# Two plain gate tiles, a delayed overwrite of an activation sum, and transposes inside the first branch, in a hybrid decoder layer

## The chip, the cores and the metric

The kernel runs on one NeuronCore of one Trainium2 chip. The metric is the device time of one execution in microseconds (us). The engines named below are PE (matrix multiplication, with PEld for its weight loads), DVE and ACT (elementwise work; both read PSUM), POOL (elementwise work on SBUF) and SP, which here only issues DMAs.

## What is computed

One inference step of one decoder layer for 1024 prompt tokens and 64 sample tokens, 1088 columns in all, with a model width of 1024. Cut to what matters here:

```
proj = rms_norm(x) @ w_in              # holds, among others, g_a and g_b (1024 columns each)
h_m  = mLSTM branch (512 wide)         h_a = sliding-window attention branch (512 wide)
mix  = sigmoid(g_a) * (h_m @ w_branch_a) + sigmoid(g_b) * (h_a @ w_branch_b)
x    = x + mix @ w_out
x    = x + (silu(hf @ w_gate) * (hf @ w_up)) @ w_down      # hf = rms_norm(x)
```

The four stages the change touches are, in order of time: the gates g_a and g_b, the merge of the two branches, and the projection by `w_out` with the preparation of the feed-forward part.

## The kernel before

Every fp32 operand is held as a high and a low part (`XH`, `XL` for the activations, `wh`, `wl` for weights), so one product is three matmuls (`product`, L158). Activations lie as [128, 8, 1088]: eight blocks of 128 features, 1088 tokens. The tokens are cut in two halves of 544 (`first`, `second`), and each half into pieces of 256 and 288 columns (`halves`).

**Gates (L1042 to L1107).** There are eight gate tiles of 128 columns, m = 0 to 7, each for both branches. Tile 0 is computed plainly: for each branch and half, two pieces of 24 matmuls, 192 in all. Tiles 1 to 7 use a seven-product scheme (Strassen's, in Winograd's form) in place of eight: `times` (L1000) issues 12 matmuls for each piece of each product, so 168 a tile. The scheme needs sums of activation blocks. With a11, a12 the two feature halves of the first token half and a21, a22 those of the second, they are S1 = a21 + a22, S2 = S1 - a11, S3 = a11 - a21 and S4 = a12 - S2. The loop at L1063 makes them in four quarters of 136 columns and splits each into high and low parts. S2 to S4 go to tiles of their own (`SH`, `SL`, shown as SHG, SLG); S1 overwrites a21 in `XH`, `XL` (L1068). That write must wait for the plain tile's reads of the same columns, and it is the first split of its quarter. `right_sides` (L978) makes seven weight sums a tile from two raw loads, and `right` (L971) splits each into a slot of the tags `wh` and `wl`, which have four slots each. A gate result goes through tanh on ACT and is stored to DRAM (`TG`).

**Merge (L1109 to L1172).** `merge_all(1)` multiplies the attention output (features 0 to 3 of `XH`) with `w_branch_b`, 8 tiles of three chunks (384, 352, 352 columns) of 12 matmuls, and DVE multiplies with the gate. Then nine tiles of the mLSTM output are loaded from DRAM (`VED`) into `ve` (three buffers), transposed on PE (four transposes each, into one of two `tp` buffers of PSUM), copied by ACT to the high part and subtracted by DVE to the low part (L1159 to L1169). `merge_all(0)` then does for the mLSTM branch what `merge_all(1)` did for the other; POOL adds the two.

**Projection and preparation (L1208 to L1310).** Each token tile is multiplied with `w_out` in four column groups of 256. For groups 2 and 3, `project_rows` (L1231) uses one PSUM tile each, one DVE add (L1209) and one ACT square with its sum (L1210). `norm_rows` (L1235), `turn` (L1264) and `combine` (L1249) follow: they normalise, transpose and make the sums of the feed-forward part's own seven-product scheme.

The order on each engine outside the two hand-ordered early parts (L561, L563) is not the order of the text. A planner sets it when the program is built: it simulates the engines in time, and takes among the instructions that it believes ready, by and large, the one earliest in the text. On the chip each engine then runs its list strictly in that order, and SP issues all DMAs from one list.

Of the kernel before, what the change touches and what calls it, by code (L numbers as in the profile page):

```python
# [9 lines left out]
F32 = mybir.dt.float32  # L10
F32R = mybir.dt.float32r
I32 = mybir.dt.int32
AF = mybir.ActivationFunctionType
ALU = mybir.AluOpType
AX = mybir.AxisListType
PSUM = bass.MemoryType.PSUM

P = 128
D = 1024
KD = D // P  # L20
# [4 lines left out]
TILES = [(t, t * P, min(P, T - t * P)) for t in range((T + P - 1) // P)]  # L25
# [49 lines left out]
def hybrid_kernel(ctx: ExitStack, tc: tile.TileContext, i, o):  # L75
# [15 lines left out]
    def f32(ap):  # L91
        return ap.bitcast(F32)
# [25 lines left out]
    def split(hi, lo, raw, pin=False):  # L118
        ins = S.copy(hi, raw)  # L119
        if pin:  # L120
            tc.keep_in_program_order(ins)
        V.tensor_tensor(lo, raw, f32(hi), op=ALU.subtract)  # L122
# [31 lines left out]
    def load_tile(w, c0, kt=8, n=P, **kw):  # L154
        hi, lo = load_w([(w_rows(w, 0, kt, c0, n), 0, n)], kt, n, **kw)
        return [(hi[:, k], lo[:, k]) for k in range(kt)]
# [36 lines left out]
    def by_feature(out, c0, cn, ws, xh, xl):  # L193
        product(out, [(ws[k], (xh[:, k, c0:c0 + cn], xl[:, k, c0:c0 + cn])) for k in range(len(ws))])
# [829 lines left out]
    def f544(a):  # L1024
        return a[:, 256:800]
# [10 lines left out]
    def gate_tiles(m):  # L1036
        return [MIX[:, x, HALF * (m % 2):HALF * (m % 2) + HALF] for x in range(4)]

    def store_gate(branch, m, h, w):
        nc.sync.dma_start(TG[branch, m, :, HALF * h:HALF * h + HALF], w)  # L1040

    ws = [load_tile(i["w_in"], c0) for c0 in (GA, GB)]  # L1042
    w4 = gate_tiles(0)
    for branch in range(2):
        for h in range(2):
            a = ag.tile([P, 1024], F32, tag="ag", name="pg")
            for cs in halves:
                by_feature(a[:, 256 + cs.start:256 + cs.stop], HALF * h + cs.start, cs.stop - cs.start, ws[branch], XH, XL)
            w = w4[2 * branch + h]
            S.activation(w, f544(a), AF.Tanh, scale=0.5)  # L1050
            store_gate(branch, 0, h, w)

    CQ = HALF // 4
    quarters = [slice(CQ * n, CQ * n + CQ) for n in range(4)]
# [1 line left out]
    def whole(q, half, cs, out=None):  # L1056
        c = slice(HALF * half + cs.start, HALF * half + cs.stop)
        if out is None:
            out = cg.tile([P, 4, CQ], F32, tag="cg", name="cg")
        V.tensor_tensor(out, f32(XH[:, q, c]), f32(XL[:, q, c]), op=ALU.add)  # L1060
        return out

    for cs in quarters:  # L1063
        c = slice(HALF + cs.start, HALF + cs.stop)
        s3 = whole(q0, 1, cs, MIX[:, 0:4, c])
        s2 = whole(q1, 1, cs)
        V.tensor_tensor(s2, s3, s2, op=ALU.add)
        split(XH[:, q0, c], XL[:, q0, c], s2)  # L1068
        a11 = whole(q0, 0, cs)
        V.tensor_tensor(s2, s2, a11, op=ALU.subtract)  # L1070
        split(SH[:, 0, :, cs], SL[:, 0, :, cs], s2)
        V.tensor_tensor(s3, a11, s3, op=ALU.subtract)
        split(SH[:, 1, :, cs], SL[:, 1, :, cs], s3)
        s4 = whole(q1, 0, cs)
        V.tensor_tensor(s4, s4, s2, op=ALU.subtract)
        split(SH[:, 2, :, cs], SL[:, 2, :, cs], s4)

    def gate_sides():
        for m in range(1, 8):
            yield from right_sides(*load_gates(m))  # L1080

    HH, HL = XH[:, q0], XL[:, q0]
    left, sides, ready = left_sides(), gate_sides(), []
    for m in range(1, 8):
        outs, (w1, w2, w3, sg) = {}, gate_tiles(m)
        for n in range(7):
            w = take_side(sides, ready)
            if BANKS[n] not in outs:
                outs[BANKS[n]] = ag.tile([P, 1024], F32, tag="ag", name="pg")
            a = outs[BANKS[n]]  # L1090
            for cs in halves:
                times(a[:, 256 + cs.start:256 + cs.stop], left[n], w, FRESH[n], cs)
            sums(n, {b: f544(x) for b, x in outs.items()}, w1, w2, w3)
            if n == 2:
                S.activation(sg, f544(a), AF.Tanh, scale=0.5)
                store_gate(0, m, 0, sg)
            elif n >= 4:
                x = (w3, w2, w1)[n - 4]
                S.activation(x, x, AF.Tanh, scale=0.5)
                store_gate(int(n < 6), m, int(n != 5), x)  # L1100
            if m == 7 and n < 2:
                for cs in quarters:
                    c = slice(HALF * n + cs.start, HALF * n + cs.stop)
                    split(HH[:, :, c], HL[:, :, c], HA[:, :, c])
# [19 lines left out]
    def merge_all(branch, xh, xl):  # L1124
        for m in range(8):
            th = gp.tile([P, T], F32, tag="gth", name="gth", bufs=4)
            nc.sync.dma_start(th[:], TG[branch, m])
            if m % 2 == 0:
                if branch:
                    raw = load_b(m * P)  # L1130
                    hi = wp.tile([P, WT], F32R, tag="wh", name="wh")
                    lo = wp.tile([P, WT], F32R, tag="wl", name="wl")
                    split(hi[:, :1024], lo[:, :1024], raw[:, :1024])
                    h3 = hi[:, :1024].rearrange("p (k n) -> p k n", k=4)
                    l3 = lo[:, :1024].rearrange("p (k n) -> p k n", k=4)
                else:
                    h3, l3 = load_w([(w_rows(i["w_branch_a"], 0, 4, m * P, 256), 0, 256)], 4, 256)
            ms = slice((m % 2) * P, (m % 2) * P + P)
            wm = [(h3[:, k, ms], l3[:, k, ms]) for k in range(4)]
            for c0, cn in CHUNKS:  # L1140
                pb = acc.tile([P, 512], F32, tag="acc", name="pb")
                by_feature(pb[:, :cn], c0, cn, wm, xh, xl)
                mx, tc_ = MIX[:, m, c0:c0 + cn], th[:, c0:c0 + cn]
                if branch:
                    V.scalar_tensor_tensor(mx, tc_, 1.0, pb[:, :cn], op0=ALU.add, op1=ALU.mult)
                else:
                    V.scalar_tensor_tensor(tc_, tc_, 1.0, pb[:, :cn], op0=ALU.add, op1=ALU.mult)
                    G.tensor_tensor(mx, mx, tc_, op=ALU.add)

    ves = []  # L1150
    for t, r0, nt in TILES:
        ve = gp.tile([P, 4, P], F32, tag="ve", name="ve", bufs=3)
        nc.sync.dma_start(ve[:nt], VED[t, 0:nt])
        ves.append(ve)
        if t == 2:
            break
    merge_all(1, HH, HL)
    HH, HL = XH[:, q1], XL[:, q1]
    for t, r0, nt in TILES:  # L1159
        if t < len(ves):  # L1160
            ve = ves[t]
        else:
            ve = gp.tile([P, 4, P], F32, tag="ve", name="ve", bufs=3)
            nc.sync.dma_start(ve[:nt], VED[t, 0:nt])
        tp = ptp.tile([P, 4, P], F32, tag="tp", name="tp")
        for h in range(4):
            PE.transpose(tp[:, h, :nt], ve[:nt, h], ident[:nt, :nt])
        S.copy(HH[:, :, r0:r0 + nt], tp[:, :, :nt])
        V.tensor_tensor(HL[:, :, r0:r0 + nt], tp[:, :, :nt], f32(HH[:, :, r0:r0 + nt]), op=ALU.subtract)  # L1169
    merge_all(0, HH, HL)  # L1170
    for c in (close_ptp, close_acc, close_gp):
        c()  # L1172

# [1 line left out]
    def col(t):  # L1175
        return t * P + (HALF - 4 * P if t >= 4 else 0)
# [54 lines left out]
    def project_rows(t, u):  # L1231
        nt = TILES[t][2]
        add_rows(t, u, wu[u - 2], x2s[t][:nt, 256 * u:256 * u + 256], nt)

    def norm_rows(t):  # L1235
        _, r0, nt = TILES[t]
        x2 = x2s.pop(t)
        ss, y, a = (np_.tile([P, 1], F32, tag=n, name=n, bufs=2)[:nt] for n in ("ns", "ny", "na"))
        V.tensor_reduce(ss, ss4[:nt, t], axis=AX.X, op=ALU.add)
        S.activation(y, ss, AF.Ln, scale=1.0 / D, bias=eps[:nt])  # L1240
        S.activation(y, y, AF.Exp, scale=-0.5)
        V.tensor_scalar(ss, ss, -0.5 / D, -0.5 * EPS, op0=ALU.mult, op1=ALU.add)
        V.tensor_scalar(a, y, y, ss, op0=ALU.mult, op1=ALU.mult)
        V.tensor_scalar(y, a, 1.5, y, op0=ALU.add, op1=ALU.mult)
        xns[t] = nq.tile([P, D], F32, tag="xn", name="xn", bufs=2)
        norm_apply(x2, xns[t], nfw, nt, y)
        nc.sync.dma_start(X2D[r0:r0 + nt, 512:D], x2[:nt, 512:D])
# [47 lines left out]
    for n, t in enumerate(rows[:7]):  # L1295
        if n + 3 < len(rows):
            load_rows(rows[n + 3])
        for u in (2, 3):
            project_rows(t, u)
        norm_rows(t)  # L1300
        if n >= 2:
            turn(rows[n - 2])
# [225 lines left out]
```

## Time and profile before

| what | value |
|---|---|
| median of 3 runs | 1528.57 us (1527.46 to 1529.47) |
| profiled execution, its own time | 1530.48 us |
| span of the profile (first to last instruction) | 1528.5 us |
| PE busy | 1470.6 us, 96% of the span, 10430 matmuls |
| DVE busy | 801.6 us, 52% |
| ACT busy | 511.6 us, 33% |
| POOL busy | 249.0 us, 16% |
| mean granted TensorE clock | 0.991 |

PE's busy share is made of modelled matmul ends and hides how densely the matmuls follow one another, so stretches are better judged by how many matmuls they hold. The profile's 40 slices are 38.2 us each. The gates run from 386.7 to 576.0 us, the merge from 576.0 to 683.1 us, the projection and the preparation from there to about 816 us.

### The profile page before, as it was taken

What the parts mean: (1) busy time and instruction counts of PE and PEld (TensorE: products, weight loads), DVE (VectorE), ACT (ScalarE), POOL (GpSimd) and SP (SyncE); (2) the same over time, 40 slices, a digit from 0 to 9 for tenths busy, and PEclk for the clock granted to TensorE, in tenths of its full rate; (3) what the DMA queues carried; (4) which work ended last, traced back from release to release, by engine and by line L of the source; (5) the groups of instructions that cost most, each with busy time, mean ns of one, the idle gap of its engine ahead of it and who ended that gap; (6) DMA issues with size and microseconds to landing.
All of it is one profiled execution on the core that took longest, in us unless ns stands there. A gap on an engine that the chain in (4) does not pass through costs nothing.

```text
span 1528.5 us, 25750 instructions
## 1 busy us (share of the span) xinstructions
PE 1470.6 (96%) x10430; PEld 1382.0 (90%) x10430; DVE 801.6 (52%) x1515; ACT 511.6 (33%) x1059; POOL 249.0 (16%) x359
## 2 busy tenths in 40 slices
PE   6999999999979999899999999999999999999998
PEld 5887799888879999899999999999999998888887
DVE  6877525477764453444596555555555563325221
ACT  5666433321333341223463222223222242224110
POOL 1211100235101100140143222112221110000000
PEclk9999999999979999999999999999999999999999
DMA  8100113112313336334422233223232246536440
GB/s 259 37 15 11 49 55 84 55 44 56 99 57 114 90 122 224 124 103 144 157 87 83 73 85 86 84 66 109 80 85 85 72 153 195 176 131 217 139 127 18
DMA packets 171372, 154.91 MB, mean 101 GB/s; under 512 B 21746, under 2 KB 145074, under 8 KB 171254
## 3 DMA queue, kind: packets, MB, share of 16 engines
q1 hardware_dynamic: 171254, 153.27, 32.6%
q8 instruction: 82, 1.34, 0.4%
q14 instruction: 36, 0.29, 0.1%
HBM read 118.55 MB, written 34.70 MB: 100 GB/s over the span
## 4 chain that ended last, share of the span: by engine, by line
PE 83%; DVE 7%; ACT 3%; DMA 3%; issue 1%; POOL 1%; SPq 0%; DVEq 0%; ACTq 0%; POOLq 0%
PE pf L1005 27%; PE pg L1005 9%; PE ad L1481 6%; PE ad L1480 6%; PE acc L161 5%; PE ad L1483 5%; PE acc L163 5%; PE acc L162 5%; PE pb L161 2%; PE pb L162 2%; PE pb L163 2%; PE po L460 1%; PE sc L408 1%; DVE wl L122 1%; ACT pp L428 1%
## 5 line engine op out<-in xcount | busy, mean ns | idle before, releaser
L161 PE MATMUL acc<-wh,XH 128*128 128x256 f32 (+1 forms) x640 | 185.6, 290 | 1.7 <-ACT va L333 1.1
L163 PE MATMUL acc<-wh,XL 128*128 128x256 f32 (+1 forms) x640 | 182.5, 285 | 0.6 <-DVE XL L1193 0.6
L162 PE MATMUL acc<-wl,XH 128*128 128x256 f32 (+1 forms) x640 | 182.4, 285 | 0.0
L119 ACT CAST wh<-raw 128x512 fp32r<-128x512 f32 (+2 forms) x108 | 81.7, 762 | 211.2 <-PE pf L1005 88.5
L1005 PE MATMUL pf<-XH,wh 128*128 128x288 f32 (+1 forms) x688 | 138.5, 289 | 1.0 <-DVE w L1018 0.9
L1005 PE MATMUL pf<-XH,wl 128*128 128x256 f32 (+1 forms) x656 | 131.9, 288 | 0.0
L161 PEld LDWEIGHTS acc<-wh,XH 128*128 128x128 f32 x640 | 123.5, 193 | 6.7 <-issue 3.9
L163 PEld LDWEIGHTS acc<-wh,XL 128*128 128x128 f32 x640 | 123.4, 193 | 0.8 <-DVE XL L1193 0.8
L162 PEld LDWEIGHTS acc<-wl,XH 128*128 128x128 f32 x640 | 123.4, 193 | 0.0
L1005 PEld LDWEIGHTS pf<-XH,wh 128*128 128x128 f32 x688 | 111.2, 189 | 1.5 <-DVE w L1018 1.5
L1005 PEld LDWEIGHTS pf<-XH,wl 128*128 128x128 f32 x656 | 106.1, 188 | 0.0
L1005 PE MATMUL pf<-SH,wl 128*128 128x288 f32 (+1 forms) x512 | 102.3, 288 | 0.0
L1005 PE MATMUL pf<-XL,wh 128*128 128x256 f32 (+1 forms) x344 | 99.3, 289 | 0.0
L1005 PE MATMUL pf<-SH,wh 128*128 128x256 f32 (+1 forms) x496 | 99.0, 288 | 0.0
L1005 PE MATMUL pf<-XL,wl 128*128 128x288 f32 (+1 forms) x328 | 94.6, 289 | 0.0
L1337 POOL TENSOR_TENSOR w<-w,w 128x544 f32<-128x544 f32 x21 | 37.4, 1781 | 299.2 <-ACT w L1336 284.7
L122 DVE TENSOR_TENSOR SL<-kraw,SH 128x1536 fp32r<-128x1536 f32 (+1 forms) x24 | 39.8, 1658 | 83.2 <-ACT SH L119 83.2
L1481 PE MATMUL ad<-XL,SH 128*128 128x512 f32 x214 | 83.3, 389 | 0.0
L1480 PE MATMUL ad<-XH,SH 128*128 128x512 f32 x214 | 83.3, 389 | 0.0
L122 DVE TENSOR_TENSOR wl<-raw,wl 128x512 fp32r<-128x512 f32 x61 | 53.2, 874 | 57.3 <-ACT wl L119 57.3
L1005 PEld LDWEIGHTS pf<-SH,wl 128*128 128x128 f32 x512 | 82.5, 189 | 0.1
L1005 PEld LDWEIGHTS pf<-SH,wh 128*128 128x128 f32 x496 | 80.0, 189 | 0.0
(423 smaller groups left out, 3824.6 us busy)
## 6 DMA issues: line engine op xcount, KB each, us to landing
raw<-in_w_in_dram SPq DMA_DIRECT2D x30, 512.0 KB
kraw<-AD SPq DMA_DIRECT2D x16, 768.0 KB
AD<-w SPq DMA_DIRECT2D x42, 256.0 KB
kraw<-AD SPq DMA_DIRECT2D x16, 640.0 KB
TG<-MIX SPq DMA_DIRECT2D x32, 272.0 KB
gth<-TG SPq DMA_DIRECT2D x16, 544.0 KB
raw<-in_w_gate_dram SPq DMA_DIRECT2D x12, 512.0 KB
raw<-in_w_up_dram SPq DMA_DIRECT2D x12, 512.0 KB
```

The costliest lines, as they stand in the source:

```text
L119: ins = S.copy(hi, raw)
L122: V.tensor_tensor(lo, raw, f32(hi), op=ALU.subtract)
L161: PE.matmul(out, lh, rh, start=(a == 0), stop=False)
L162: PE.matmul(out, lh, rl, start=False, stop=False)
L163: PE.matmul(out, ll, rh, start=False, stop=(a == n - 1))
L408: PE.matmul(scs[kv][:, g, :nb], qt[64 * kv:64 * kv + 64, 2 * gp + g, :], KT[64 * kv:64 * kv + 64, k0:k0 + nb], start=True, stop=True)
L428: S.activation(pp[:, g, :nb], pp[:, g, :nb], AF.Exp, bias=mx[:, 2 + g:3 + g], accum_out=mx[:, 6 + g:7 + g])
L1005: PE.matmul(out, l, r[:, k, cs], start=fresh and k == 0 and a == 0, stop=k == 3 and a == 2, skip_group_check=True)
L1337: G.tensor_tensor(w3, w3, w1, op=ALU.mult)
L1480: PE.matmul(a[:], hi[:, k], wh, start=one, stop=False)
L1481: PE.matmul(a[:], hi[:, k], wl, start=False, stop=end and nt < P)
L1483: PE.matmul(a[:], lo[:, k], wh, start=False, stop=end)
```

## The change

1. The plain gate code becomes a function `plain_gates(m)`, called for m = 0 and m = 1; the seven-product tiles are now m = 2 to 7. Within a plain tile the second token half now comes before the first, and both branches of a half follow each other. Both plain tiles write their results to the first half of the rows of `MIX`.
2. S1 is kept in `MIX[:, 0:4, second]`. S2, S3 and S4 are made and split ahead of `plain_gates(1)` in the text; the split of S1 into `XH`, `XL`, which overwrites a21, stands behind it.
3. The transposes of the mLSTM output become `turn_ve(t)`, called inside `merge_all(1)`, behind the matmuls of the first chunk of each tile m = 1 to 7: tile m - 1, and at m = 7 also tiles 7 and 8. Its loads are issued there too.
4. `project_both(t)` makes column groups 2 and 3 in the two halves of one PSUM tile, with one DVE add and one ACT square over 512 columns. It serves token tiles 0, 4, 1, 5, 2 and 6; the sample tile and tiles 3 and 7 stay as they were. The sum of squares then adds three columns instead of four.

```diff
-    ws = [load_tile(i["w_in"], c0) for c0 in (GA, GB)]
-    w4 = gate_tiles(0)
-    for branch in range(2):
-        for h in range(2):
-            a = ag.tile([P, 1024], F32, tag="ag", name="pg")
...
+    def plain_gates(m):
+        ws = [load_tile(i["w_in"], c0 + m * P) for c0 in (GA, GB)]
+        for h in (1, 0):
+            for branch in range(2):
+                a = ag.tile([P, 1024], F32, tag="ag", name="pg")
+                for cs in halves:
+                    by_feature(a[:, 256 + cs.start:256 + cs.stop], HALF * h + cs.start, cs.stop - cs.start,
+                               ws[branch], XH, XL)
+                w = gate_tiles(0)[2 * branch + h]
+                S.activation(w, f544(a), AF.Tanh, scale=0.5)
+                store_gate(branch, m, h, w)
...
+    plain_gates(0)
+    S1 = MIX[:, 0:4, second]
+    for cs in quarters:
+        a21, a22 = whole(q0, 1, cs), whole(q1, 1, cs)
+        V.tensor_tensor(S1[:, :, cs], a21, a22, op=ALU.add)
+        a11 = whole(q0, 0, cs)
+        V.tensor_tensor(a22, S1[:, :, cs], a11, op=ALU.subtract)
+        split(SH[:, 0, :, cs], SL[:, 0, :, cs], a22)
+        V.tensor_tensor(a21, a11, a21, op=ALU.subtract)
+        split(SH[:, 1, :, cs], SL[:, 1, :, cs], a21)
+        a12 = whole(q1, 0, cs, a11)
+        V.tensor_tensor(a12, a12, a22, op=ALU.subtract)
+        split(SH[:, 2, :, cs], SL[:, 2, :, cs], a12)
+    plain_gates(1)
     for cs in quarters:
         c = slice(HALF + cs.start, HALF + cs.stop)
-        s3 = whole(q0, 1, cs, MIX[:, 0:4, c])
-        s2 = whole(q1, 1, cs)
-        V.tensor_tensor(s2, s3, s2, op=ALU.add)
-        split(XH[:, q0, c], XL[:, q0, c], s2)
...
+        split(XH[:, q0, c], XL[:, q0, c], S1[:, :, cs])
 
     def gate_sides():
-        for m in range(1, 8):
+        for m in range(2, 8):
             yield from right_sides(*load_gates(m))
...
-    for m in range(1, 8):
+    for m in range(2, 8):
         outs, (w1, w2, w3, sg) = {}, gate_tiles(m)
...
                 if branch:
+                    if c0 == 0 and m:
+                        turn_ve(m - 1)
+                        if m == 7:
+                            turn_ve(7)
+                            turn_ve(8)
                     V.scalar_tensor_tensor(mx, tc_, 1.0, pb[:, :cn], op0=ALU.add, op1=ALU.mult)
...
+    def turn_ve(t):
+        _, r0, nt = TILES[t]
         ve = gp.tile([P, 4, P], F32, tag="ve", name="ve", bufs=3)
         nc.sync.dma_start(ve[:nt], VED[t, 0:nt])
...
         tp = ptp.tile([P, 4, P], F32, tag="tp", name="tp")
         for h in range(4):
             PE.transpose(tp[:, h, :nt], ve[:nt, h], ident[:nt, :nt])
-        S.copy(HH[:, :, r0:r0 + nt], tp[:, :, :nt])
-        V.tensor_tensor(HL[:, :, r0:r0 + nt], tp[:, :, :nt], f32(HH[:, :, r0:r0 + nt]), op=ALU.subtract)
-    merge_all(0, HH, HL)
+        S.copy(HH2[:, :, r0:r0 + nt], tp[:, :, :nt])
+        V.tensor_tensor(HL2[:, :, r0:r0 + nt], tp[:, :, :nt], f32(HH2[:, :, r0:r0 + nt]), op=ALU.subtract)
+
+    merge_all(1, HH, HL)
+    merge_all(0, HH2, HL2)
...
+    def project_both(t):
+        nt = TILES[t][2]
+        a = acc.tile([P, 512], F32, tag="acc", name="acc")
+        for u in range(2):
+            out = a[:, 256 * u:256 * u + 256]
+            product(out, [((XH[:, k, col(t):col(t) + P], XL[:, k, col(t):col(t) + P]), wu[u][k]) for k in range(KD)])
+        xs = x2s[t][:nt, 512:D]
+        V.tensor_tensor(xs, a[:], xs, op=ALU.add)
+        S.activation(junk[:nt], xs, AF.Square, accum_out=ss4[:nt, t, 2:3])
...
-        for u in (2, 3):
-            project_rows(t, u)
+        if t == NCT:
+            project_rows(t, 2)
+            project_rows(t, 3)
+        else:
+            project_both(t)
```

## Rows read from the trace of the kernel before

**Rows 1.** The page, 40 slices: busy tenths of PE, and the granted clock.
```profile
PE   6999999999979999899999999999999999999998
...
PEclk9999999999979999999999999999999999999999
```

**Rows 2.** Windows, gate matmuls alone: stretch, length, busy (count), clock, DMA share, GB/s.
```profile
413.95:440.00 26.05, 13.26 (x73) 0.67 0.07 20
440.00:576.04 136.04, 136.04 (x1083) 1.00 0.38 114
386.60:576.04 189.44, 176.59 (x1368) 0.95 0.32 99
```

**Rows 3.** Timeline of PE, plain tile 0: start, length, line, operation; piece boundaries.
```profile
398.83 0.28 PE L161 MATMUL pg<-XH,wh 128*128 128x256 f32 x1
...
401.69 0.30 PE L161 MATMUL pg<-XH,wh 128*128 128x288 f32 x1
...
404.86 0.28 PE L161 MATMUL pg<-XH,wh 128*128 128x256 f32 x1
```

**Rows 4.** Timeline of PE, tile 1: matmuls after idle time, with its releaser.
```profile
415.74 0.39 PE L1005 MATMUL pg<-XL,wl 128*128 128x256 f32 x1 [1.56 <-DVE XL L122]
...
420.86 0.39 PE L1005 MATMUL pg<-SLG,wl 128*128 128x256 f32 x1 [1.89 <-DVE SLG L122]
...
431.13 0.61 PE L1005 MATMUL pg<-XH,wl 128*128 128x288 f32 x1 [8.08 <-ACT XH L119]
```

**Rows 5.** Windows, all engines: PE, PEld, DVE, ACT, POOL busy (count), clock, DMA.
```profile
422.00:424.00 2.00, 1.04 (x5) 0.75 (x4) 2.00 (x5) 0.65 (x1) 0.00 (x0) 0.50 0.00 0
...
438.00:440.00 2.00, 2.00 (x16) 2.00 (x16) 0.49 (x1) 0.62 (x1) 0.74 (x1) 0.85 0.00 0
...
390.81:436.41 45.60, 32.81 (x236) 31.70 (x235) 38.38 (x55) 17.48 (x29) 4.62 (x3) 0.84 0.15 49
```

**Rows 6.** Timeline of DVE and POOL around tile 0 and the first quarter of sums.
```profile
382.99 1.22 DVE L122 TENSOR_TENSOR wl<-raw,wh 128x1024 fp32r<-128x1024 f32 x1 [1.08 <-ACT wh L119]
...
388.55 1.29 DVE L122 TENSOR_TENSOR wh<-raw,wh 128x512 fp32r<-128x512 f32 x2 [1.48 <-ACT wh L119]
...
390.81 3.09 DVE L1060 TENSOR_TENSOR cg<-XH,XL 128x544 f32<-128x544 f32 x3
...
396.54 1.85 DVE L122 TENSOR_TENSOR SLG<-MIX,SHG 128x544 fp32r<-128x544 f32 x1 [0.16 <-ACT SHG L119]
...
396.51 1.29 POOL L989 TENSOR_TENSOR raw<-raw 128x512 f32<-128x512 f32 x1 [3.83 <-ACT SHG L119]
```

**Rows 7.** One group of DVE by line, 390.81 to 436.41: busy, mean ns, idle before.
```profile
L122 DVE TENSOR_TENSOR XL<-cg,XH 128x544 fp32r<-128x544 f32 x4 | 2.9, 719 | 5.8 <-ACT XH L119 5.8
```

**Rows 8.** Windows of the merge, columns as in the windows of all engines.
```profile
576.04:623.60 47.56, 47.56 (x290) 47.54 (x289) 17.44 (x28) 4.76 (x5) 0.00 (x0) 1.00 0.58 198
...
576.04:683.10 107.06, 102.09 (x615) 99.92 (x614) 42.80 (x66) 15.73 (x21) 22.26 (x23) 0.98 0.46 152
```

**Rows 9.** Timeline of PE, the transposes between the branches.
```profile
623.60 1.04 PE L1167 MATMUL tp<-ident,ve 128*128 128x128 f32 x8
...
626.61 1.25 PE L1167 MATMUL tp<-ident,ve 128*128 128x128 f32 x8 [1.97 <-DVE XL L1169]
...
633.36 1.94 PE L1167 MATMUL tp<-ident,ve 128*128 128x128 f32 x8 [2.11 <-DMA ve<-VED]
```

**Rows 10.** Windows just behind the last wait, columns as before.
```profile
634.00:636.00 2.00, 1.94 (x9) 1.34 (x8) 0.74 (x2) 1.17 (x2) 0.00 (x0) 0.50 0.14 16
```

**Rows 11.** The end of the preparation: its window, two groups of DVE, one wait of PE.
```profile
798.00:816.00 18.00, 12.73 (x98) 12.07 (x97) 16.73 (x26) 10.41 (x19) 10.11 (x7) 1.00 0.12 36
...
L1209 DVE TENSOR_TENSOR x<-acc,x 128x256 f32<-128x256 f32 x16 | 6.6, 418 | 8.3 <-DMA x<-in_x_prompt_dram 5.0 <-PE acc L163 3.2
...
L1254 DVE TENSOR_TENSOR s<-tp,a 128x512 f32<-128x512 f32 x4 | 2.7, 681 | 0.6 <-ACT a L1253 0.6
...
PE tp L241 <- DVE xn L234: 2.5, 1, 2.5
```

More of the change, by code (lines that the diff above doesn't have):

```diff
@@ L1040, in store_gate @@
         nc.sync.dma_start(TG[branch, m, :, HALF * h:HALF * h + HALF], w)
-    ws = [load_tile(i["w_in"], c0) for c0 in (GA, GB)]
-    w4 = gate_tiles(0)
-    for branch in range(2):
-        for h in range(2):
-            a = ag.tile([P, 1024], F32, tag="ag", name="pg")
[L1047 to L1051, printed above, removed]
+    def plain_gates(m):
[9 more added lines that the diff above has]
+                store_gate(branch, m, h, w)
     CQ = HALF // 4
@@ L1061, in whole @@
         return out
+    plain_gates(0)
[12 more added lines that the diff above has]
+    plain_gates(1)
     for cs in quarters:
         c = slice(HALF + cs.start, HALF + cs.stop)
-        s3 = whole(q0, 1, cs, MIX[:, 0:4, c])
-        s2 = whole(q1, 1, cs)
-        V.tensor_tensor(s2, s3, s2, op=ALU.add)
-        split(XH[:, q0, c], XL[:, q0, c], s2)
[L1069 to L1076, printed above, removed]
+        split(XH[:, q0, c], XL[:, q0, c], S1[:, :, cs])
     def gate_sides():
-        for m in range(1, 8):
+        for m in range(2, 8):
             yield from right_sides(*load_gates(m))
@@ L1148, in merge_all @@
                     G.tensor_tensor(mx, mx, tc_, op=ALU.add)
-    ves = []
-    for t, r0, nt in TILES:
+    HH2, HL2 = XH[:, q1], XL[:, q1]
+    def turn_ve(t):
+        _, r0, nt = TILES[t]
         ve = gp.tile([P, 4, P], F32, tag="ve", name="ve", bufs=3)
         nc.sync.dma_start(ve[:nt], VED[t, 0:nt])
[L1154 to L1164, printed above, removed]
         tp = ptp.tile([P, 4, P], F32, tag="tp", name="tp")
@@ L1238, in norm_rows @@
         ss, y, a = (np_.tile([P, 1], F32, tag=n, name=n, bufs=2)[:nt] for n in ("ns", "ny", "na"))
-        V.tensor_reduce(ss, ss4[:nt, t], axis=AX.X, op=ALU.add)
+        V.tensor_reduce(ss, ss4[:nt, t, 0:4 if t in (3, 7, NCT) else 3], axis=AX.X, op=ALU.add)
         S.activation(y, ss, AF.Ln, scale=1.0 / D, bias=eps[:nt])
```

## The prediction

> **What bounds the kernel now.** I read the page's 40 slices first. The reader is to see that PE stands at 9 nearly everywhere, so PE's list sets the time, and that the exceptions after the start lie in slice 12 (420 to 458 us, where the clock shows 7 too), slice 17 (611 to 649 us) and slices 21 and 22 (764 to 840 us) [rows 1]. These are the three places where the change works. I then read each by windows, which give the number of matmuls in a stretch, and by PE's timeline, which names what PE waited for.
>
> Where the gates run undisturbed, 1083 matmuls take 136.04 us, 0.1256 us each [rows 2]. The timeline agrees: 24 matmuls of 256 columns take 2.86 us and 24 of 288 columns 3.17 us [rows 3]. Between 413.95 and 440.00 only 73 were done in 26.05 us [rows 2]. They were worth 73 x 0.1256 = 9.2 us, so 16.9 us were lost there. The gates as a whole took 189.4 us for 1368 matmuls worth 171.8, so 0.7 us is lost elsewhere. PE waited 1.56, 1.89 and 8.08 us, the longest for the write of S1 into XH [rows 4]; the granted clock then stood at 0.50, the 1.2 GHz level, and was back near 1 only in the window from 438 [rows 5].
>
> Why PE waits is seen on DVE. It was busy 38.4 of the 45.6 us from 390.81 to 436.41 [rows 5], and its one long idle time, 5.8 us, is for the same write [rows 7]: S1 overwrites columns that the plain tile still reads, and all later sums queue behind it. So tile 1 starts on PE before its activation sums exist.
>
> **Part 1, the gates.** Removed: one seven-product tile, 168 x 0.1256 = 21.1 us of PE. Added: one plain tile, 192 x 0.1256 = 24.1 us. PE's own work grows by 3.0 us. The Trainium skill (TensorE: Matmul & The Clock Gate, Back-to-back issue gap) gives an isolated gap of the columns divided by 2.4 GHz plus 2.5 ns, that is 109 and 122.5 ns; by it the 24 extra matmuls would be an estimated 2.8 us, but the trace shows 119 and 132 ns here [rows 3], and the trace decides.
>
> What the 3.0 us buy is cover. Plain tile 0 runs from 386.6 to 410.8, plain tile 1 then to 434.9, and neither needs a sum. S2 to S4 wait for no reader any more. DVE's work from 390.8 on: 48 sum and split instructions, about six weight instructions of tile 2 (its slots come free at about 405, 411, 429 and 435, so four sides and two weight sums), at the 38.4 / 55 = 0.70 us that an instruction took [rows 5], 37.8 us, and two plain weight splits of 1.22 us [rows 6], together 40.2 us. It ends near 431, inside the 44.1 us of cover, with 3.9 us to spare. If that cover were gone, each further us would be a us of PE.
>
> The new wait is the write of S1. It stands behind plain tile 1's reads of the second half, which now come first and end at 410.8 + 12.05 = 422.9. Queued behind it on DVE and ACT are tile 2's weight splits and the tanh of tile 1; PE needs S1 only in the second product of tile 2, near 438. Four splits at 0.72 us [rows 7] end near 427. Tile 1's two raw loads are the same as before: the first had landed by 388.55, when DVE worked on it, ahead of the first sum at 390.81 [rows 6]. I take the same order now, so the plain splits are done near 393, long before 410.8. The loads for tile 2 can then be issued earlier than before, since a raw buffer is held for one split, not for four sides. Stores keep their number, four a tile, and sit on the same SP list.
>
> What remains as a stall at 434.9 the trace does not show. At the low end it is nothing; at the high end it is one slow DVE split, 1.85 us [rows 6]. I take 1.0, since margin exists but is thin. Gain: 16.9 - 3.0 - 1.0 = 12.9 us, between 12.0 and 14.6 (all of the 17.6, less 3.0).
>
> **Part 2, the transposes.** A branch of 288 matmuls takes 47.56 us when undisturbed [rows 8], so two take 95.1. The first eight transposes took 1.04 us [rows 9], 0.13 each, so 36 are 4.7 us. The sum is 99.8 us, and the merge took 107.06 [rows 8]: 7.3 us are lost. The timeline says on what: DVE returning a tp buffer (1.97 us) and a load of ve (2.11 us) [rows 9], then the clock at 0.50 [rows 10]. Nine tiles in a row share two tp and three ve buffers with nothing beside them. In the change they come one every 5.9 us (47.56 / 8), between matmuls. DVE is busy 17.4 of 47.56 us and ACT 4.8 there [rows 8], so both copies hide. Each moved step also issues a load. On SP it stands among the gate loads that wait for their own buffers; the next tile is wanted 5.9 us later with three buffers in hand, and the DMA engines are at 0.58 [rows 8]. PE still pays the 4.7 us. At m = 7 three tiles meet two buffers: between nothing, if the second chunk goes first, and the 1.97 us seen. I take 0.5, as two chunks are left to run. Gain 6.8 us, between 5.3 and 7.3. What is late next is nothing in this stage: branch 0 starts with all but the last tiles in place.
>
> **Part 3, one tile for two column groups.** Two adds of 0.418 become one near 0.68, which is what 512 columns out of PSUM take [rows 11]: 6 x 0.16 = 0.9 us less on DVE, and an add that ends 0.26 us later after its last matmul, 1.6 us over six tiles at worst. The stall of this stage is behind those tiles: in 798 to 816 PE was busy 12.7 of 18.0 us, and its longest wait, 2.5 us, is for the normalised rows of the last tile [rows 11], whose code is unchanged. I take 0, with bounds of 0.9 gained and 1.6 lost.
>
> **Sum.** 12.9 + 6.8 + 0 = 19.7 us. The profiled execution took 1530.48 us, 1.9 above the median of the runs; from it the sum gives 1510.8, from the median of 1528.57 it gives 1508.9. I predict for the median: **1508.9 us**.
>
> **The rivals.**
>
> *DVE becomes the bound of the gates.* If the planner puts tile 1's plain splits behind the 44 sums, DVE reaches them at 390.8 + 44 x 0.70 = 421.6, and PE, out of work at 410.8, waits until about 422.8. That is 12 us, and with the clock's fall about 3 more (it stayed down for some 6 us of work before, [rows 5]). The gates then gain 12.9 - 15 = -2 us and the time is 1524. Against it: in the trace weight splits went ahead of the sums [rows 6]. For it: a DVE split beside a POOL subtraction of 1.29 us took 1.85 us in place of 0.72 [rows 6, 7]. The Trainium skill (SBUF — State Buffer, Who interferes with whom) says that a DVE instruction with two SBUF inputs and a POOL instruction that reads SBUF lock each other out for a whole instruction; by that rule these sums are the kind that suffers, and the trace agrees with 1.85 us. 0.08.
>
> *The transposes don't move.* If the planner believes the ve loads late, it leaves the transposes where they are. The second part gains nothing: 1515.7. For it: a load of ve was waited for [rows 9]. 0.12.
>
> *The preparation is planned anew and worse.* Its list of DVE is full (16.7 of 18.0 us), and a second stall of the size of the present 5.3 us [rows 11] gives 1514.2. 0.06.
>
> *Slower: PE's list waits for a load at every turn.* A transpose fixed in PE's list ahead of its load stops the chunks behind it. One wait of 2.11 us [rows 9] was followed by about 4 us at a lower clock [rows 10], worth 2.0 more. Seven such turns cost 28.8 us: the merge takes 128.6 in place of 107.1, and with the gates' 12.9 gained the time is 1537. It decides from where the turns lose more than the two parts win, 7.3 + 12.9 = 20.2 us, or 2.9 us a turn. Against it: three buffers and 5.9 us a turn. 0.04.
>
> **How the numbers follow.** The forecast has 0.70, the others as given. The forecast's own bounds are 12.0 to 14.6, 5.3 to 7.3 and -1.6 to 0.9, so 15.7 to 22.8 us gained, 1505.8 to 1512.9. The range takes in the second and third rivals at the top, and 2 us at the bottom for a better order in the preparation, which holds 5.3 us of idle time: 1504 to 1516.5. The measurement can tell a change from none at about 0.2%, 3 us. All cases but the last are faster by more; I leave 0.03 for a first rival that costs a little more, and 0.05 for slower in all, so 0.92 for faster.
>
> **What would show it.** Right: no PE wait over 2 us and a clock of 1.00 between 386 and 580 us; the gate matmuls count 1392 and take about 176 us; the first branch about 52 us with 36 transposes in it and the second 47.6, with no window of clock below 1. Wrong: a PE wait for wh or wl at about 411 (first rival), transposes still bunched (second), waits for ve at each turn (slower), or idle time in the preparation that differs from 5.3 us by more than 2.

## The result and the profile after

The changed kernel took 1506.93 us, median of 4 runs (1504.43 to 1507.47), beside 1529.02 us for the kernel before (the three runs told of above and one more): a ratio of 0.985, 95% interval 0.9831 to 0.9869. The forecast was 1508.9 with 1504 to 1516.5. The profiled execution after took 1507.47 us, its span 1505.7 us.

I cut both spans at the first gate matmul, the first merge matmul, the end of the last one, the first matmul of the feed-forward part and the first of its down projection:

| stage, us | before | after | after - before |
|---|---|---|---|
| up to the gates (code unchanged) | 386.7 | 383.8 | -2.9 |
| gates | 189.3 | 175.2 | -14.1 |
| merge | 107.1 | 99.2 | -7.9 |
| projection and preparation | 135.3 | 136.1 | +0.8 |
| feed-forward products (code unchanged) | 445.2 | 446.5 | +1.3 |
| down projection (code unchanged) | 264.9 | 264.9 | 0 |

The page after, its 40 slices (busy tenths of PE, granted clock), answers [rows 1]. The weak slices 12 and 17 are gone; slice 21, in the preparation, is the one that is left.

```profile
PE   6999999999999999999989999999999999999998
...
PEclk9999999999999999999999999999999999999999
```

Windows of the gate matmuls alone (stretch, length, busy with count, clock, DMA share, GB/s) answer [rows 2]. There are 1392 matmuls in place of 1368. They fill 175.19 of 175.23 us at a clock of 1.00: 0.126 us each, the undisturbed pace, throughout.

```profile
383.80:432.00 48.20, 48.16 (x382) 1.00 0.30 95
432.00:559.03 127.03, 127.03 (x1012) 1.00 0.36 112
383.80:559.03 175.23, 175.19 (x1392) 1.00 0.35 107
```

DVE in the same stretch (timeline: start, length, line, operation, idle time before and its releaser) answers [rows 6, 7]. The plain splits of tile 1 come at 386.04 and 389.47, the first ahead of all sums, the second behind their first three additions. S1 goes into XL at 417.10 and 420.73, while plain tile 1 runs, and holds up nobody. The last sum is split at 425.97, a weight split of tile 2 ends at 428.7, and then DVE is idle for 4.33 us while PE still has plain work until about 432.

```profile
386.04 1.23 DVE L122 TENSOR_TENSOR wl<-raw,wh 128x1024 fp32r<-128x1024 f32 x1 [1.80 <-ACT wh L119]
387.56 2.00 DVE L1061 TENSOR_TENSOR cg<-XH,XL 128x544 f32<-128x544 f32 x3 [0.29 <-DMA VED<-VE]
389.47 1.22 DVE L122 TENSOR_TENSOR wl<-raw,wh 128x1024 fp32r<-128x1024 f32 x1
390.61 0.71 DVE L1068 TENSOR_TENSOR MIX<-cg 128x544 f32<-128x544 f32 x1
...
417.10 0.71 DVE L122 TENSOR_TENSOR XL<-MIX,XH 128x544 fp32r<-128x544 f32 x1
...
420.73 1.98 DVE L122 TENSOR_TENSOR XL<-MIX,XH 128x544 fp32r<-128x544 f32 x3
...
425.97 0.73 DVE L122 TENSOR_TENSOR SLG<-cg,SHG 128x544 fp32r<-128x544 f32 x1 [0.71 <-ACT SHG L119]
...
428.05 0.69 DVE L122 TENSOR_TENSOR wl<-raw,wl 128x512 fp32r<-128x512 f32 x1 [0.34 <-ACT wl L119]
433.07 0.69 DVE L122 TENSOR_TENSOR wh<-raw,wh 128x512 fp32r<-128x512 f32 x1 [4.33 <-ACT wh L119]
```

The merge by windows of all engines (PE, PEld, DVE, ACT, POOL busy with count, clock, DMA share, GB/s) answers [rows 8]; the second window holds the end of the first branch and the beginning of the other.

```profile
559.03:606.60 47.57, 47.57 (x302) 47.36 (x301) 20.91 (x34) 8.09 (x12) 0.00 (x0) 1.00 0.68 224
606.60:611.00 4.40, 4.40 (x29) 4.08 (x29) 2.20 (x4) 1.36 (x3) 0.00 (x0) 1.00 0.04 15
559.03:658.20 99.17, 99.17 (x615) 98.64 (x614) 42.61 (x66) 14.82 (x20) 22.27 (x23) 1.00 0.52 171
```

PE's timeline of the transposes answers [rows 9]: four at a time, one token tile every 6.4 us, no idle time in front of any, the last twelve of the 36 between 605 and 611 us.

```profile
567.05 0.60 PE L1167 MATMUL tp<-ident,ve 128*128 128x128 f32 x4
...
573.40 0.60 PE L1167 MATMUL tp<-ident,ve 128*128 128x128 f32 x4
...
605.21 1.04 PE L1167 MATMUL tp<-ident,ve 128*128 128x128 f32 x8
...
610.37 0.47 PE L1167 MATMUL tp<-ident,ve 64*128 64x64 f32 x4
```

The waits of PE in the projection and the preparation (what waited, for what: us in all, times, longest) answer the last row of [rows 11]. They add up to 5.3 us, where the kernel before has 5.9 (2.5, 2.1, 0.7 and 0.6): 2.5 for the normalised rows has become 1.8, and the others stand about where they did.

```profile
PE acc L1005 <- DVE x L1015: 2.1, 1, 2.1
PE tp L241 <- DVE xn L234: 1.8, 1, 1.8
PE acc L1005 <- ACT x L1013: 0.8, 1, 0.8
PE acc L163 <- DVE XL L1195: 0.6, 1, 0.6
```

### The profile page after: what moved, and what is told of

It is laid out like the page before. It is cut to its first block, busy times and chain, and to the rows that moved or that the text cites. A ratio compares the mean times of both kernels' runs of the same rounds, so it can differ in the third digit from the quotient of the medians.

```text
span 1505.7 us, 25751 instructions
## 1 busy us (share of the span) xinstructions
PE 1466.9 (97%) x10454; PEld 1381.1 (92%) x10454; DVE 794.6 (53%) x1497; ACT 507.1 (34%) x1041; POOL 252.5 (17%) x357
## 4 chain that ended last, share of the span: by engine, by line
PE 86%; DVE 5%; ACT 3%; DMA 3%; issue 2%; SPq 1%; POOL 0%; DVEq 0%; ACTq 0%; POOLq 0%
PE pf L1005 27%; PE pg L1005 8%; PE ad L1495 6%; PE ad L1496 6%; PE acc L161 5%; PE ad L1498 5%; PE acc L163 5%; PE acc L162 5%; PE pb L163 2%; PE pb L162 2%; PE pb L161 2%; PE pg L161 1%; PE pg L163 1%; PE pg L162 1%; PE po L460 1%
## 5 line engine op out<-in xcount | busy, mean ns | idle before, releaser
L1005 PE MATMUL pf<-XH,wl 128*128 128x288 f32 (+1 forms) x688 | 138.5, 288 | 1.8 <-DVE w L1018 1.7
L1005 PE MATMUL pf<-XH,wh 128*128 128x256 f32 (+1 forms) x656 | 131.9, 288 | 0.0
L119 ACT CAST wh<-raw 128x512 fp32r<-128x512 f32 (+2 forms) x96 | 75.2, 789 | 116.2 <-PE pb L162 45.4
L1005 PEld LDWEIGHTS pf<-XH,wh 128*128 128x128 f32 x656 | 106.0, 188 | 0.0
L1005 PE MATMUL pf<-SH,wh 128*128 128x288 f32 (+1 forms) x512 | 102.3, 288 | 0.4 <-DVE w L1015 0.4
L1005 PE MATMUL pf<-XL,wl 128*128 128x256 f32 (+1 forms) x344 | 99.1, 288 | 0.0
L1005 PE MATMUL pf<-SH,wl 128*128 128x256 f32 (+1 forms) x496 | 99.0, 288 | 0.0
L1005 PE MATMUL pf<-XL,wh 128*128 128x288 f32 (+1 forms) x328 | 94.5, 288 | 0.0
L122 DVE TENSOR_TENSOR wh<-raw,wh 128x512 fp32r<-128x512 f32 x58 | 51.9, 897 | 59.2 <-ACT wh L119 59.2
L119 ACT CAST wl<-raw 128x512 fp32r<-128x512 f32 x68 | 42.2, 621 | 120.4 <-PE pf L1005 88.1
```

What stands on the lines that cost most here:

```text
L1005: PE.matmul(out, l, r[:, k, cs], start=fresh and k == 0 and a == 0, stop=k == 3 and a == 2, skip_group_check=True)
```

## The experiments

Each ratio is against the kernel before, run beside it on the same chip: 1528.33 us in the median for e0 to e3, 1526.77 for e4 to e7, 1528.67 for e8 to e10. Diffs are against the changed kernel. The last three columns are stages of the profiled execution, in us.

| run | what it is | median us | ratio, 95% | gates | merge | preparation |
|---|---|---|---|---|---|---|
| e0_after | the change again | 1505.48 | 0.9838 to 0.9867 | 175.2 | 99.2 | 134.5 |
| e1_gates | part 1 alone | 1512.37 | 0.9882 to 0.9915 | 175.1 | 105.4 | 135.2 |
| e2_turns | part 2 alone | 1521.26 | 0.9941 to 0.9971 | 189.1 | 99.2 | 135.6 |
| e3_no_both | without part 3 | 1505.98 | 0.9841 to 0.9870 | 175.2 | 99.2 | 135.8 |
| e4_one_plain | one plain tile, S1 last | 1512.10 | 0.9886 to 0.9916 | 181.3 | 99.2 | 135.6 |
| e5_old_sums | two plain tiles, S1 first | 1508.96 | 0.9858 to 0.9891 | 175.2 | 99.2 | 136.0 |
| e6_first_first | first half first | 1508.07 | 0.9855 to 0.9887 | 175.2 | 99.2 | 136.1 |
| e7_bunched | transposes in one bunch | 1514.12 | 0.9892 to 0.9926 | 175.2 | 108.0 | 136.1 |
| e8_three_plain | three plain tiles | 1508.08 | 0.9857 to 0.9890 | 178.3 | 99.2 | 134.0 |
| e9_lo_dve | low parts on DVE | 1508.94 | 0.9862 to 0.9891 | 175.1 | 99.2 | 138.9 |
| e10_lo_mixed | half of them on DVE | 1507.16 | 0.9849 to 0.9878 | 175.2 | 99.2 | 134.6 |

### Which part gave what

**e0_after** is the changed kernel, unedited, beside the next three.

> The changed kernel again, beside the runs below on one chip. All theories expect 1507 us, 22 below the kernel before.

**e1_gates** puts the transposes back between the branches, with their loads, and takes `project_both` out.

```diff
-                    if c0 == 0 and m:
-                        turn_ve(m - 1)
...
+    merge_all(1, HH, HL)
+    HH, HL = XH[:, q1], XL[:, q1]
+    for t, r0, nt in TILES:
...
+    merge_all(0, HH, HL)
...
```

> The kernel before with the first part alone (second plain gate tile, S1 written last). Theory of additive parts: the gates take 175.2 us in place of 189.4 and nothing else moves, so 14 us less than before, about 1515. Rival, that the transposes between the branches take over part of the wait once the gates end earlier: the merge grows beyond 107 us and the time is 1518 or more.

**e2_turns** keeps the moved transposes and puts back the gates of the kernel before and `project_rows`.

```diff
-    plain_gates(0)
...
-    plain_gates(1)
...
+        s3 = whole(q0, 1, cs, MIX[:, 0:4, c])
...
+        split(XH[:, q0, c], XL[:, q0, c], s2)
...
```

> The kernel before with the second part alone (transposes inside the first branch). Theory of additive parts: the merge takes 99.1 us in place of 107.1 and nothing else moves, so 8 us less than before, about 1521. Rival, that the loads are late without the earlier end of the gates: the merge keeps a wait of 2 us or more and the time is 1523 to 1529.

**e3_no_both** takes only `project_both` out.

```diff
...
-        if t == NCT:
-            project_rows(t, 2)
-            project_rows(t, 3)
-        else:
-            project_both(t)
+        for u in (2, 3):
+            project_rows(t, u)
```

> The changed kernel without its third part (column groups 2 and 3 each in their own PSUM tile, as before). Theory that the third part is worth nothing: the same as the changed kernel within 1 us, 1507. Rival, that the third part lengthened the preparation (135.3 us before, 136.1 us after, from the first matmul of the projection to the first of the block loop) by an add that ends later: 1 to 2 us less than the changed kernel, 1505 to 1506. Second rival, that it saves DVE work that counts: 1 us or more above it.

Measured: 1505.48, 1512.37, 1521.26 and 1505.98 us beside 1528.33. Part 1 alone gains 16.0 us, part 2 alone 7.1, the two in one kernel (e3) 22.4, all three (e0) 22.9. They add up within the noise, so neither hides the other. e2's PE waits in the gates are those of before (7.8 us for the high part of S1, 2.8 in two for its low part, 1.7 for another sum), so the transposes have no hand in the gates. Part 3 can't be told from nothing: e0's and e3's intervals overlap nearly whole, and their runs span 1504.95 to 1507.02 and 1504.89 to 1508.14.

In e1, PE's waits in the merge show what is left of [rows 9] when only the gates change; its merge takes 105.4 us against 107.1, since the wait for a load has shrunk from 2.1 to 0.5. So beside part 1 the move of the transposes is worth 105.4 - 99.2 = 6.2 us in the merge, and without part 1 107.1 - 99.2 = 7.9.

```profile
PE tp L1171 <- DVE XL L1173: 2.0, 1, 2.0
...
PE tp L1171 <- DMA ve<-VED: 0.5, 1, 0.5
PE pb L161 <- ACT XH L1172: 0.5, 1, 0.5
```

### What in part 1 does it: the second plain tile or the late S1

**e4_one_plain** keeps S1 last, but has only one plain tile.

```diff
-    plain_gates(1)
...
-        for m in range(2, 8):
+        for m in range(1, 8):
             yield from right_sides(*load_gates(m))
...
-    for m in range(2, 8):
+    for m in range(1, 8):
```

> The changed kernel with one plain gate tile only (tiles 1 to 7 by seven products); S1 is still kept apart and written last. Theory that the second plain tile's cover is what counts: PE's work falls by 3.0 us, but the plain tile ends near 408 and the first product near 411, while DVE's sums ran to 427 in the changed kernel; PE waits 8 to 14 us for them and the clock falls, so 1512 to 1520. Rival, that writing S1 last is enough by itself: no wait, 1503 to 1505.

**e5_old_sums** keeps two plain tiles and makes the sums in the order of the kernel before, S1 first and into XH at once, behind both plain tiles in the text.

```diff
     plain_gates(0)
-    S1 = MIX[:, 0:4, second]
...
     plain_gates(1)
     for cs in quarters:
...
-        split(XH[:, q0, c], XL[:, q0, c], S1[:, :, cs])
+        s3 = whole(q0, 1, cs, MIX[:, 0:4, c])
+        s2 = whole(q1, 1, cs)
+        V.tensor_tensor(s2, s3, s2, op=ALU.add)
+        split(XH[:, q0, c], XL[:, q0, c], s2)
...
```

> The changed kernel with both plain tiles first and then the old order of the sums (S1's split first in its quarter). Theory that the order of the overwrite counts too: the first split of S1 waits for the second plain tile's reads until about 416, most of the 44 other sums stand behind it and end 30 us later, PE is out of work at 435 and waits 8 to 15 us with a fall of the clock: 1514 to 1524. Rival, that 48 us of cover are enough in any order: 1505 to 1508.

**e6_first_first** turns the order of the halves inside a plain tile back, so that a21 is read last.

```diff
-        for h in (1, 0):
+        for h in (0, 1):
```

> The changed kernel with the first token half ahead of the second in the plain tiles. By my margins: the reads of the second half end with the second plain tile at 432 in place of 420, the four writes of S1 end near 434, and PE wants S1 at 435, so nothing to 2 us is lost, 1505 to 1508. Rival, that the turned halves are needed: a wait for S1 of 3 us or more with a fall of the clock, 1509 to 1514.

Measured, e4: 1512.10 us, gates 181.3. With one plain tile fewer PE has 3.1 us less to do (e8, below), so undisturbed they would take 172.1; 9.2 us were lost, in place of 189.3 - 172.1 = 17.2 in the kernel before. S1 made last, with the halves turned so that a21 is read first, is worth 8.0 us there; the two were not parted behind one plain tile. The rest of the stall stands in PE's timeline, for the same write as in [rows 4], and in windows of all engines, DVE busy 33.7 of 34 us ahead of it, 21.3 of 23.4 around it, and the clock at 0.50 behind it:

```profile
420.74 0.61 PE L1005 MATMUL pg<-XH,wl 128*128 128x288 f32 x1 [5.68 <-ACT XH L119]
...
421.94 0.61 PE L1005 MATMUL pg<-XL,wl 128*128 128x288 f32 x1 [0.59 <-DVE XL L122]
```

```profile
386.00:420.00 34.00, 29.06 (x232) 28.85 (x231) 33.67 (x51) 13.92 (x23) 6.98 (x3) 1.00 0.22 70
407.61:431.00 23.39, 17.12 (x116) 16.59 (x115) 21.28 (x33) 10.21 (x17) 9.64 (x2) 0.85 0.22 67
420.00:422.00 2.00, 0.67 (x2) 0.35 (x2) 2.00 (x5) 0.65 (x1) 2.00 (x1) 0.50 0.00 0
```

Here S1's write isn't held up by a reader: DVE was simply not yet there. It was busy nearly all the time from 386 to 420, while the plain tile had ended near 408, and made the last quarter of S1 only at 419.3. The idle 5.8 us of [rows 7] are gone, and a stall stays.

e5 went against my theory: gates of 175.2 us, to the tenth those of the change, and 1508.96 us where I had put 1514 or more. Its PE waits in the whole stretch from 386 to 563 us are this one line, the start of the stage:

```profile
PE pg L161 <- ACT th L928: 0.5, 1, 0.5
```

And yet the sums on DVE did stand still for the write of S1: between 396.6 and 419.3 there is none, with idle times of 9.06 us (until a weight cast of ACT, the next thing that was ready) and of 4.97 us, and the last sum was split only at 451.5. DVE's timeline:

```profile
405.66 0.69 DVE L122 TENSOR_TENSOR wh<-raw,wh 128x512 fp32r<-128x512 f32 x1 [9.06 <-ACT wh L119]
...
419.29 0.72 DVE L122 TENSOR_TENSOR XL<-cg,XH 128x544 fp32r<-128x544 f32 x1 [4.97 <-ACT XH L119]
...
443.42 0.72 DVE L122 TENSOR_TENSOR XL<-cg,XH 128x544 fp32r<-128x544 f32 x1
...
447.80 0.72 DVE L122 TENSOR_TENSOR SLG<-cg,SHG 128x544 fp32r<-128x544 f32 x1
...
450.75 0.71 DVE L122 TENSOR_TENSOR SLG<-cg,SHG 128x544 fp32r<-128x544 f32 x1
```

PE's list shows why that costs nothing. Its first matmul on S2 to S4 stands at 439.55 and takes 256 columns, that is the first two quarters; the first one on the other 288 columns comes at 449.23:

```profile
449.23 0.29 PE L1005 MATMUL pg<-SHG,wh 128*128 128x288 f32 x1
```

This isn't the list of the change: the planner drew PE's list up anew for e5. In the change the 288 columns of a product stand right behind its 256, those of S1 (the second product) from about 436.86 and those of S2 from about 442.90:

```profile
436.86 0.29 PE L1005 MATMUL pg<-XL,wl 128*128 128x288 f32 x1
...
442.90 0.29 PE L1005 MATMUL pg<-SLG,wl 128*128 128x288 f32 x1
```

The plain work ends at 432.3 in the change, so these are 4.6 and 10.6 us behind its end. In e5 it ends at 435.1, and the same list would want these columns at 439.7 and 445.7, while the last quarter of S1 was written until 444.1 and that of S2 until 448.5. By the list of the change PE would have waited some 4 us (an estimate from these rows). e5's list sets other products before them, and nothing is lost.

So behind two plain tiles the order of the sums is worth nothing that the gates show, once PE's list is planned for it, and behind one it is worth 8.0 us, with the halves turned. The late S1 is needless beside the second plain tile, which with the halves turned brings all 14.1 us. A kernel with two plain tiles, S1 first and the halves in their old order wasn't run. e5's median is 2.0 us above the change's own and 3.5 above e0's, and its interval overlaps e0's only at the edge (0.9858 to 0.9867); of the 4.1 us between the two spans, 3.6 lie ahead of the gates (386.7 us against 383.1), where the code is the same.

e6 shows the same from another side: its gates take 175.2 us too, with no PE wait over 0.5 us, and it ran in 1508.07 us. S1 is written 12 to 13 us later than in the change, as its reader ends later (and the gates begin 1.7 us later), and that is not felt. DVE's timeline in e6:

```profile
430.30 0.72 DVE L122 TENSOR_TENSOR XL<-MIX,XH 128x544 fp32r<-128x544 f32 x1
...
433.25 2.00 DVE L122 TENSOR_TENSOR XL<-MIX,XH 128x544 fp32r<-128x544 f32 x3 [2.23 <-ACT XH L119]
```

**e8_three_plain** measures the price of a plain tile by itself, where there is no stall left to win.

```diff
     plain_gates(1)
+    plain_gates(2)
...
-        for m in range(2, 8):
+        for m in range(3, 8):
```

> The changed kernel with a third plain gate tile. Theory: no wait is left in the gates, so nothing more can be hidden, and the tile costs its 24 extra matmuls at 0.1256 us, 3.0 us: 1508.5 beside 1505.5 for the changed kernel, with the gates at 178.2 us. Rival, that some hidden slowness of the seven-product tiles (weight sums that come late) goes too: 1507 or less.

Measured: gates 178.3 us, 3.1 more than with two, 1508.08 us. The windows of the gate matmuls show 24 more of them at the same full clock:

```profile
381.90:560.20 178.30, 178.26 (x1416) 1.00 0.35 105
```

That is 3.07 us, 128 ns for each of 24, beside 0.1256 us in [rows 2]: the 3.0 us of the sum. The isolated gap of the Trainium skill (TensorE: Matmul & The Clock Gate, Back-to-back issue gap), an estimated 2.8 us for them, is again a little short.

### What in part 2 does it: the place or the spreading

**e7_bunched** leaves all nine token tiles inside the first branch, but turns them at once, at m = 7.

```diff
-                    if c0 == 0 and m:
-                        turn_ve(m - 1)
-                        if m == 7:
-                            turn_ve(7)
-                            turn_ve(8)
+                    if c0 == 0 and m == 7:
+                        for t in range(9):
+                            turn_ve(t)
```

> The changed kernel with all nine transposed tiles called at the last tile of the first branch, so inside the branch but bunched. Theory that spreading them is what counts, since nine tiles share two PSUM and three SBUF buffers: two chunks of 1.9 us are the only cover, and 3 to 7 of the 7.9 us come back, 1509 to 1513. Rival, that it is enough that the text has them ahead of the second branch: 1505 to 1507.

Measured: merge 108.0 us, no better than before, 1514.12 us. PE's timeline of the transposes and one window behind the longest wait:

```profile
602.90 1.04 PE L1165 MATMUL tp<-ident,ve 128*128 128x128 f32 x8
...
610.62 0.66 PE L1165 MATMUL tp<-ident,ve 128*128 128x128 f32 x4 [0.94 <-DVE XL L1167]
...
618.70 1.00 PE L1165 MATMUL tp<-ident,ve 128*128 128x128 f32 x4 [3.97 <-DMA ve<-VED]
```

```profile
620.00:622.00 2.00, 2.00 (x8) 2.00 (x8) 0.69 (x1) 0.32 (x1) 0.00 (x0) 0.50 0.00 0
```

It lost 8.8 us against the change: 6.2 us of waits (3.97 for a load into one of three `ve` buffers, 0.94 for DVE, 1.3 in three for ACT's copies) and, by subtraction, 2.6 at the lower clock. The gain of part 2 is the spreading: with a tile every 6.4 us each buffer is free again and each load has landed before it is wanted. The place in the text is worth nothing by itself.

### What holds the preparation

Of the stages that the change touches, the preparation has the most idle time left, so I tried there. **e9_lo_dve** moves the subtractions that make the low parts of the feed-forward sums from POOL to DVE; **e10_lo_mixed** moves those of two of the four column blocks.

```diff
-            G.tensor_tensor(lo, x, f32(hi), op=ALU.subtract)
+            V.tensor_tensor(lo, x, f32(hi), op=ALU.subtract)
```

> The changed kernel with the low-part subtractions of the preparation's sums on DVE in place of POOL (the line in combine). A POOL subtraction of 1.5 us was seen to stretch a DVE split from 0.7 to 1.8 us. Theory that this is what makes DVE late at the end of the preparation: 16 fewer POOL instructions free some 16 x 1.1 us of DVE and cost 16 x 0.68, the idle time of PE behind the last tile shrinks by 1 to 4 us, and the time is 1502 to 1505. Rival, that DVE's own count of work decides: 16 more instructions of 0.68 us make the end 3 to 8 us later, 1508 to 1513.

```diff
-            G.tensor_tensor(lo, x, f32(hi), op=ALU.subtract)
+            (V if c in (2 * P, 3 * P) else G).tensor_tensor(lo, x, f32(hi), op=ALU.subtract)
```

> The same, but only for the last two pairs of token tiles; the first two pairs and the sample tile stay on POOL. By the first theory most of the gain is kept, 1502 to 1505, since only the end is on the path; by the rival half of the loss, 1506 to 1509.

Measured, e9: 1508.94 us with a preparation of 138.9, longer and not shorter, so my theory fell. One subtraction is quicker on DVE, in e9:

```profile
L1273 DVE TENSOR_TENSOR SL<-s,SH 128x512 fp32r<-128x512 f32 x6 | 4.0, 681 | 0.0
```

than on POOL in the change (both in 770 to 794 us):

```profile
L1273 POOL TENSOR_TENSOR SL<-s,SH 128x512 fp32r<-128x512 f32 x4 | 6.5, 1635 | 0.0
```

But the sixteen of 512 columns are 10.9 us more on an engine that was nearly full (four more of 128 columns are small). In windows of all engines, 770 to 794 us, DVE is busy 21.34 of 24 us in the change (first fence) and 23.73 in e9 (second), and PE did 136 matmuls there and 118; both stretches hold some time at the lower clock:

```profile
770.00:794.00 24.00, 19.34 (x136) 18.47 (x135) 21.34 (x36) 11.43 (x22) 10.45 (x8) 0.93 0.23 66
```

```profile
770.00:794.00 24.00, 17.76 (x118) 16.65 (x116) 23.73 (x42) 14.26 (x27) 4.44 (x3) 0.86 0.11 31
```

The Trainium skill (SBUF — State Buffer, Who interferes with whom) says that a DVE instruction with two SBUF inputs and a POOL instruction that reads SBUF contend. By that rule taking the work off POOL frees DVE; the 1.85 us of [rows 6] agree with the rule, yet freeing DVE of it was worth less here than the 10.9 us that it took on: over the whole preparation DVE is busy 94.05 us in e9 and 90.37 in the change. That this is what lengthens the preparation isn't shown, as PE's longest wait there, 2.4 us, is for a weight cast of ACT in a list planned anew. e10 came out at 1507.16 us, between the change and e9, with a preparation of 134.6 us as in e0, and its interval overlaps that of the change: nothing won.

No kernel tried was faster than the change by more than its own runs differ.

## Why the prediction was right

**The bound and the two stalls.** The forecast of 1508.9 was 2.0 us too high. The two stages that I named gave 14.1 + 7.9 = 22.0 us in the profiles, where the sum had 19.7. The profiles differ by 22.8, and the 0.8 left over is -2.9 + 0.8 + 1.3 in stages that the change hardly touches. One reading was wrong: slices 21 and 22 stand at 9 in [rows 1] and are no exceptions there; the idle time of the preparation is seen in the windows of [rows 11] alone.

**Part 1, 12.9 forecast, 14.1 seen.** The terms were: 16.9 lost, 3.0 for 24 matmuls, 1.0 for what remains. The second held (3.1 in e8). The third was nothing: of the 17.6 us that the gates of before stood above their matmuls, only the 0.5 at the start of the stage is left, 17.6 - 3.0 - 0.5 = 14.1. DVE's work was sized well: from 386 to 432 us it was busy 40.65 us,

```profile
386.00:432.00 46.00, 46.00 (x367) 46.00 (x366) 40.65 (x58) 18.31 (x31) 9.63 (x2) 1.00 0.27 85
```

where I had 40.2 from 390.8 on, ending near 431. The gates began 2.9 us earlier than before, so my 431 stands for 428.1 here; it ended at 428.7. The order was also nearly as I took it, the plain splits ahead of all but three additions of the sums, so the first rival never came about.

What failed in this part is the step on the margin, "3.9 us to spare" and "each further us would be a us of PE". In e5 the sums ended at 451.5, some 20 us past my 431 and 16 past the end of the cover, and PE lost nothing. The change itself never tried the step, as DVE had 3.6 us to spare there. I had treated the end of the plain work as the due time of all the sums. It is the due time of none: each piece has its own, up to 10.6 us and more behind that end in the change, and the planner can put it off further, as it did in e5. Since the due times lie behind the plain work, the step "PE needs S1 near 438" and the one on the halves' order (422.9) decided nothing, as e6 shows. And I put down the stall of before to two causes at once, DVE's volume and the 5.8 us that S1 blocked it. e4 and e5 price them: with one plain tile the late S1 and the turned halves are worth 8.0 of 17.2 us, with two the late S1 is worth nothing.

**Part 2, 6.8 forecast, 7.9 seen.** 36 transposes cost 99.2 - 95.1 = 4.0 us, 0.11 each, not the 0.13 of the first eight, and nothing was left at m = 7, where I had 0.5. The mechanism, buffers that come free too slowly in a bunch, is what e7 shows. The rival in which the transposes stay and the slower one, in which each turn waits for its load, left no trace: PE has no wait for `ve` at all.

**Part 3, 0 forecast.** e3 bears it out as far as it can be measured.

**The rival of a worse preparation.** It took 0.8 us more, with 5.3 us of waits beside 5.9 before (the 5.3 of the forecast was the idle time of one window of 18 us). In e0, the same kernel, it took 134.5 us, so the 0.8 is not the plan's (see below).

**What is not settled.** The -2.9 us ahead of the gates I put down to chance, as the stage takes 381.9 to 386.7 us in the runs after, with the same code. In the profile of before, two windows there show a clock of 0.79; the row of one of them, and of the same stretch after:

```profile
360.00:368.00 8.00, 8.00 (x54) 7.34 (x53) 3.48 (x14) 1.64 (x5) 4.66 (x26) 0.79 0.34 88
```

```profile
360.00:368.00 8.00, 8.00 (x67) 7.34 (x66) 5.28 (x18) 1.66 (x6) 6.76 (x28) 1.00 0.31 73
```

That fits, but no run was made to force it. What would shorten the preparation wasn't found.

## What to carry to other kernels

When a bottleneck engine starves because its operands are prepared too late, first ask which of its own work needs no preparation, and do more of that first: 3.1 us of extra matmuls bought off 17 us of stall here. Size the cover by the due time of each piece, not by the end of the covering work; where a planner orders the consumer's list, read the due times from the list of the kernel at hand, since the next edit may move them. Test edits that aim at one stall one by one, since one may make the other needless. A serial bunch on few buffers is best spread out among work that doesn't use them.

## What the runs showed of the hardware

The same idle time is not always followed by a fall of the clock. In the profile of the change PE's wait of 2.1 us near 789 us is followed by a window at the 1.2 GHz level; in e0, the same program with the same wait, it is not. Windows of all engines, the change first, then e0:

```profile
788.00:790.00 2.00, 0.50 (x3) 0.53 (x4) 1.97 (x4) 0.11 (x1) 0.44 (x1) 0.91 0.00 0
790.00:792.00 2.00, 2.00 (x10) 2.00 (x10) 0.81 (x2) 0.00 (x0) 0.00 (x0) 0.50 0.15 44
```

```profile
790.00:792.00 2.00, 2.00 (x17) 2.00 (x16) 1.40 (x4) 0.62 (x1) 0.00 (x0) 1.00 0.49 141
```

The preparation takes 136.1 us with the fall and 134.5 without. The four runs of the change go with it: 1504.43 us at a mean clock of 1.000, and 1506.79 to 1507.47 at 0.996 to 0.998. Differences of 2 us between versions of this kernel say nothing for that reason, and I have read none from the medians alone.
